# A Trainium2 kernel for one hybrid decoder layer: the heads' stage of the in-projection written out in source order on every engine

## The chip, the cores and the metric

The kernel runs on one core of a Trainium2 chip, as one program. The metric is the device time of one execution in microseconds (us). Before the change three runs took 2206.68 to 2209.07 us, median 2207.49.

The engines are TensorE (PE, matmuls, with PEld for loading its weights), VectorE (DVE), ScalarE (ACT), GpSimd (POOL) and SyncE (SP, which here only issues transfers). Each engine works through its own instructions in their order and waits where an operand isn't there yet.

## What is computed

One layer of a decoder in float32, for a prompt of 512 new tokens and 8 sample tokens that continue older sequences (520 columns in all). D_MODEL is 2048; there are 8 delta heads of dimension 128, and a pooling group 1024 wide. The reference, cut:

```python
proj = rmsnorm(h, norm_mix) @ w_in                 # [q | k | v | z | beta, decay | pool]
qkv_c, new_conv = short_conv(conv_buf, qkv, conv_w)    # 4 taps, then silu
q = l2norm(q) * 128 ** -0.5;  k = l2norm(k)
beta = sigmoid(b_raw);  g = -exp(a_log) * softplus(a_raw + dt_bias)
...
# prompt, in chunks of tokens, per head:
decay = exp(gc_i - gc_j), lower triangle
a_mat = strict_lower((k * beta) @ k.T * decay) + I
u = solve(a_mat, v * beta);  w = solve(a_mat, k * beta * exp(gc))
for each chunk:
    v_new = u - w @ S
    o = (q * exp(g)) @ S + (q @ k.T * decay) @ v_new
    S = S * exp(g_last) + k_dec.T @ v_new
# samples: the same rule token by token, from a given state
dn_out = rmsnorm(o, dn_norm) * silu(z)
pool_out = multiscale_pool(p) @ w_pool * pool_scale
h = h + concat(dn_out, pool_out) @ w_out
h = h + (silu(gate) * up) @ w_down                 # of rmsnorm(h, norm_ffn)
```

## The kernel before

**The products.** A float32 product is taken as three passes over rounded parts (`hi`, and the rest `lo`): hi by hi, hi by lo, lo by hi. The weights come in granules of 128 x 1024 (half of one tile of 128 output columns). `granule` (line 123) loads one by SP into `raw`, ACT rounds it to `hi` (line 135), DVE subtracts to get `lo` (line 137). `product` (line 174) multiplies one tile of weights by all 520 columns in 16 steps of 6 matmuls (lines 170 to 172); the finished sums are taken out of PSUM by DVE in two parts of 264 and 256 columns (`normed_out`, line 261).

**The stages.** First x is loaded, normalized and turned, then come the k tiles 8 to 13 as plain products, the k tiles 14 and 15 and the z tiles 24 to 27 by Strassen's scheme (`strassen`, lines 295 and 301 to 303), then the *heads' stage*: the tiles q h and v 16+h for heads h = 0 to 7, the other z tiles, and eight tiles of the pooling group, one after the other by `product`. In the profile that stage goes from about 172 to 640 us. Behind it follow the out-projection and the feed-forward part.

**What runs beside the products.** After every step of a product `weave.step()` gives a turn to generators in two tracks (class `Weave`, line 43); each yields a number of steps that it wants to wait. The tasks are:

- `states()` (line 1088): rows of the older state, turned by PE and convolved for the samples.
- `keys(h)` (line 1206): of head h the decay `dm` (line 1195, four parts, and Exp), k k^T and the turned k on PE, squares and a power for the norm (line 1203), the matrix `nn` (line 1230; its tile is a row of `mixa` or `mixb`) and `kd` (line 1232).
- `eliminate()` (line 1255): the triangular systems of all heads in one: the diagonal blocks of nn go to DRAM (`nn_d`) and come back as `nb`, one system per partition; 31 pairs of a product and a subtraction on DVE (lines 1269 and 1271), then a turned copy `ut` (line 1274), and both results go to DRAM (`ud_d`, lines 1272 and 1275). `load_u(h)` (line 1187) fetches those of one head as `utf`.
- `delta(h)` (line 1284): from nn and utf to the chain over the chunks: `xp` (line 1304), copy `xt_`, three iterations for `uu` (lines 1323 and 1325), then per chunk `W` (a copy on ACT, line 1365), the products with the state `S` (lines 1354, 1369, 1373) and the output. The q and v of the next head are loaded from DRAM (`c_d`) and convolved while it runs (`take_qv`).
- `gate` (line 1404), and for the samples `sample_norms`, `sample_product(h)` (line 1449; its matmuls, line 1457, read the older state `s`), `sample_out`.

A *convolution* (line 481) is a load, a first product on ACT (line 491), three taps on DVE (line 494) and a silu on ACT (line 496).

**What sets the order.** In the heads' stage PE alone has the order of the source (`manual_schedule(engines={PE})`, line 1028). The other engines' instructions are placed by a scheduler, by priorities; the weights' loads and cuts have a raised one (line 140). The convolutions of heads 2 to 5's keys are placed by hand in the Strassen stage (`early`, `slots`, `after`, line 987), those of 0, 1, 6 and 7 in the heads' stage. `delta(0)` is added to the weave 58 steps behind the start of the elimination (line 1281), each later delta one step behind the one before. The gates of all tokens are worked out in ten pieces in the plain stage (`gates(step)`, line 862); piece 8 is a matmul (line 929) on what DVE writes in piece 7 (`ds_`, line 925, in `mixa`'s room).

## Time and profile before

| | |
|---|---|
| median of three runs | 2207.49 us (2206.68 to 2209.07) |
| the profiled execution | 2204.74 us, its span 2203.0 us, mean granted clock 0.995 |
| PE | 2138.5 us busy, 97% of the span |
| DVE | 1773.2 us, 80% |
| ACT | 960.2 us, 44% |
| POOL | 479.6 us, 22% |

The span goes from the first to the last recorded instruction. The profile gives, for any stretch of it, the busy time of each engine and the granted TensorE clock (1.00 is full speed), and for every instruction what released it: a wait is written as the engine that waits, its operation and line, an arrow, and the engine, tile and line that ended the wait. Line numbers are those of the kernel before.

### The profile page before, as it was taken

To read this page: it belongs to the slowest core of one execution; us is meant where nothing else is said; L and a number is where in the kernel's file an instruction comes from. 1 tells how busy PE (TensorE), PEld (TensorE's weight loads), DVE (VectorE), ACT (ScalarE), POOL (GpSimd) and SP (SyncE) were. 2 spreads that over 40 slices of the span, in tenths; PEclk is the share of its full clock that TensorE was granted. 3 is DMA by queue.
4 is the path that set the end of the run, shared out by engine and by line. 5 is a ranking of instruction groups with operands and counts; after the bars stand their busy time and mean duration, and the time that the engine had idled before them with its cause. 6 is when DMAs were issued, how large, how long until landed. Compare 5 with 4: busy or idle time off the path is not lost.

```text
span 2203.0 us, 43043 instructions
## 1 busy us (share of the span) xinstructions
PE 2138.5 (97%) x17737; PEld 2124.9 (96%) x17737; DVE 1773.2 (80%) x2612; ACT 960.2 (44%) x1470; POOL 479.6 (22%) x600
## 2 busy tenths in 40 slices
PE   7998979999999999999999999999999999999998
PEld 7998979999999999999999999999999999999998
DVE  7788665665569989988888888888887788887997
ACT  6346514443235545443343343443433444435544
POOL 2014312121002210333323323323012402103100
PEclk9999989999999999999999999999999999999999
DMA  8246634432434552554554555555445846447333
GB/s 278 81 139 182 184 112 133 116 107 68 122 107 144 160 159 73 161 152 138 160 154 130 160 153 155 148 149 158 126 119 172 276 107 180 138 109 237 94 109 116
DMA packets 445601, 317.51 MB, mean 144 GB/s; under 512 B 23260, under 2 KB 419957, under 8 KB 442061
## 3 DMA queue, kind: packets, MB, share of 16 engines
q1 hardware_dynamic: 420941, 224.18, 36.3%
q0 software_dynamic: 23296, 89.84, 12.6%
q8 instruction: 139, 2.28, 0.4%
q10 hardware_dynamic: 1168, 0.74, 0.1%
q14 instruction: 57, 0.47, 0.1%
HBM read 261.97 MB, written 53.40 MB: 143 GB/s over the span
## 4 chain that ended last, share of the span: by engine, by line
PE 78%; DVE 10%; DMA 4%; ACT 3%; issue 2%; POOL 1%; ACTq 0%; SPq 0%; DVEq 0%; POOLq 0%
PE dn L301 21%; PE dn L302 21%; PE dn L303 21%; PE mm L170 3%; PE mm L172 3%; PE mm L171 3%; DVE lo L295 2%; DMA vT<-c_d 1%; DVE y L494 1%; ACT hi L294 1%; DVE lo L137 1%; DMA st<-a_d 1%; DVE raw L323 1%; PE dn L1323 0%; DMA mixa<-c_d 0%
## 5 line engine op out<-in xcount | busy, mean ns | idle before, releaser
L294 ACT CAST hi<-raw 128x1024 fp32r<-128x1024 f32 (+1 forms) x447 | 453.2, 1028 | 441.0 <-DVE raw L323 211.1
L295 DVE TENSOR_TENSOR lo<-raw,hi 128x1024 fp32r<-128x1024 f32 (+1 forms) x447 | 558.4, 1268 | 103.1 <-ACT hi L294 101.4
L170 PE MATMUL mm<-xh,hi 128*128 128x264 f32 (+1 forms) x960 | 290.2, 302 | 5.5 <-DVE ext L261 3.4
L172 PE MATMUL mm<-xh,lo 128*128 128x264 f32 (+1 forms) x960 | 272.2, 284 | 1.1 <-DVE lo L137 1.1
L171 PE MATMUL mm<-xl,hi 128*128 128x264 f32 (+1 forms) x960 | 272.0, 283 | 1.3 <-DVE xl L611 1.1
L170 PEld LDWEIGHTS mm<-xh,hi 128*128 128x128 f32 x960 | 182.1, 190 | 6.2 <-DVE ext L261 3.6
L171 PEld LDWEIGHTS mm<-xl,hi 128*128 128x128 f32 x960 | 182.3, 190 | 1.9 <-DVE xl L611 1.9
L323 DVE TENSOR_TENSOR raw<-raw 128x1024 f32<-128x1024 f32 (+1 forms) x136 | 182.2, 1340 | 2.3
L172 PEld LDWEIGHTS mm<-xh,lo 128*128 128x128 f32 x960 | 181.3, 189 | 1.6 <-DVE lo L137 1.6
L302 PE MATMUL dn<-b21l,hi 128*128 128x260 f32 x620 | 175.9, 284 | 0.4 <-DVE b21l L2063 0.4
L303 PE MATMUL dn<-b21h,lo 128*128 128x260 f32 x620 | 175.6, 283 | 0.0
L303 PE MATMUL dn<-b11h,lo 128*128 128x260 f32 x612 | 173.3, 283 | 2.2 <-DVE lo L295 2.2
L301 PE MATMUL dn<-b21h,hi 128*128 128x260 f32 x620 | 175.2, 283 | 0.0
L302 PE MATMUL dn<-b11l,hi 128*128 128x260 f32 x612 | 173.5, 284 | 0.0
L301 PE MATMUL dn<-b11h,hi 128*128 128x260 f32 x612 | 172.9, 283 | 0.0
L301 PE MATMUL dn<-T1h,hi 128*128 128x260 f32 x556 | 158.3, 285 | 0.0
L1685 POOL TENSOR_TENSOR mixa<-mixa 128x520 f32<-128x520 f32 x22 | 51.3, 2332 | 490.7 <-DVE mixa L1679 490.7
L302 PE MATMUL dn<-T1l,hi 128*128 128x260 f32 x556 | 158.0, 284 | 0.0
L303 PE MATMUL dn<-T1h,lo 128*128 128x260 f32 x556 | 156.9, 282 | 0.0
L301 PE MATMUL dn<-B22h,hi 128*128 128x260 f32 x548 | 156.1, 285 | 0.0
L302 PE MATMUL dn<-B22l,hi 128*128 128x260 f32 x548 | 155.9, 284 | 0.0
L303 PE MATMUL dn<-B22h,lo 128*128 128x260 f32 x548 | 154.7, 282 | 0.4 <-DVE lo L295 0.4
(737 smaller groups left out, 6942.0 us busy)
## 6 DMA issues: line engine op xcount, KB each, us to landing
raw<-in_w_gate_up_dram SPq DMA_DIRECT2D x134, 512.0 KB
raw<-in_w_in_dram SPq DMA_DIRECT2D x75, 512.0 KB
a_d<-mixa POOLq DMA_DIRECT2D x22, 1040.0 KB, 5.5
raw<-in_w_down_dram SPq DMA_DIRECT2D x48, 448.0 KB
mixb<-in_w_gate_up_dram SPq DMA_DIRECT2D x41, 512.0 KB
raw<-in_w_out_dram SPq DMA_DIRECT2D x25, 512.0 KB
st<-a_d POOLq DMA_DIRECT2D x49, 260.0 KB, 6.5
raw<-in_w_down_dram SPq DMA_DIRECT2D x24, 512.0 KB
```

Source lines behind the costliest of these rows:

```text
L137: dve.tensor_tensor(lo[:, r], raw[:, r], hi[:, r].bitcast(F32), op=ALU.subtract)
L170: te.matmul(acc[ci], wh, hi[k][:, c0:c1], start=(i == 0), stop=False)
L171: te.matmul(acc[ci], wh, lo[k][:, c0:c1], start=False, stop=False)
L172: te.matmul(acc[ci], wl, hi[k][:, c0:c1], start=False, stop=(i == len(w) - 1))
L294: act.copy(hi, raw)
L295: dve.tensor_tensor(lo, raw, hi.bitcast(F32), op=ALU.subtract)
L301: te.matmul(acc, wh[:, k, :], xf[:, k, :], start=start and k == 0, stop=False)
L302: te.matmul(acc, wh[:, k, :], xg[:, k, :], start=False, stop=False)
L303: te.matmul(acc, wl[:, k, :], xf[:, k, :], start=False, stop=stop and k == wh.shape[1] - 1)
L323: dve.tensor_tensor(r[name], r[a], r[b], op=op)
L494: return lambda: dve.scalar_tensor_tensor(ys[0], x[:, i:i + SEQ], cw(i, t), ys[0], op0=ALU.mult, op1=ALU.add)
L1685: pool.tensor_tensor(q[:, 4:8:2, :], q[:, 1:4:2, :], q[:, 0:2, :], op=ALU.subtract)
```

## The change

1. **Source order on every engine** for the heads' stage up to its 23rd tile: `manual_schedule()` without a list of engines. The last five pooling tiles stay as they were.
2. **A clock for tasks.** `Weave` gets `at(step, task)`, a task that starts at a given step (a step is six matmuls of a product), and `feed`, called at every step.
3. **Weights by step.** Granule n is used from step 8n on; its load is issued at step 8(n−3), its cut (hi on ACT, lo on DVE) at step 8n−10.
4. **Keys as staged tasks**, from the steps in `KS`, about 11 apart: each with its own convolution, then decay, silu and Exp, matmuls, squares, power, nn, with yields between. The early convolutions in the Strassen stage go. The blocks are stored by SP and fetched into `nb` head by head (`nd_d`), not by POOL in two halves.
5. **The elimination** starts at step 104 and is spread with yields over about 40 steps; the results of head 0 are stored first, `load_u(0)` comes four steps behind.
6. **Deltas** from step 154 (`D0`), 26 steps each, one behind the other. The load of the next head's q is issued at the start of a delta, that of v two steps later; Exp of dm comes behind the copy xt_. The gate is a task of its own.
7. **Samples:** `sample_product` takes 6 steps per head in place of 8. **Gates:** pieces 8 and 9 come one step later.
8. `kept_d` holds nn of heads 4 to 7 too, the decay rows are loaded ahead (`load_decay`), and some buffers are shared differently (pooling's `pw` and splits).

The diff, cut to its core:

```diff
+KS, ELIM, D0 = (-5, 8, 21, 33, 44, 55, 66, 77), 104, 154
...
     def step(self):
         self.now += 1
+        if self.feed:
+            self.feed(self.now)
+        for x in list(self.single):
+            if self.now >= x[0]:
+                n = next(x[1], None)
...
             elif step == 8:
+                pass
+            elif step == 9:
                 te.matmul(bank("e")[:, 0:128], ones[:NB, :], ds_.rearrange("p a b -> p (a b)"), start=True, stop=True)
...
+        def feed(now):
+            if (now + 10) % 8 == 0 and (now + 10) // 8 >= 2:
+                feed_cut((now + 10) // 8)
+            if now % 8 == 0:
+                feed_load(now // 8 + 3)
...
-        early = [convolution(places(h)[0], 8 + h, lambda k=k: mixa[:, 6 + k % 2, 0:SEQ]) for k, h in enumerate((2, 3, 4, 5))]
...
         def keys(h):
             x, nn = places(h)
             kT = x[:, 3:3 + SEQ]
+            conv = convolution(x, 8 + h, y_tile)
+            conv[0]()
+            load_decay(h)
+            yield 5
+            for f in conv[1:4]:
+                f()
+                yield 1
+            conv[4]()
+            yield 1
             _, dm = decay(h)
+            yield 1
+            conv[5]()
+            act.activation(dm, dm, AF.Exp)
+            yield 3
             gp_ = pst()
...
+            yield 2
             ss = d1tile("ss", [P, NCH], "ss")
             squares(ktp, ss)
+            yield 2
...
-            pool.dma_start(nn_d[:, NCH * h:NCH * h + NCH], nn.rearrange("p (n r j) -> p n r j", n=NCH, r=4))
+            for q in range(4):
+                r = slice(32 * q, 32 * q + 32)
+                sp.dma_start(nd_d[h, q].rearrange("c s j -> s c j"), nn3[r, :, r])
...
+            yield 4
+            if not nbs:
+                nbs.append(d1tile("nb", [P, 32, 32], "nb"))
+            sp.dma_start(nbs[0][16 * h:16 * h + 16].rearrange("p s j -> p (s j)"),
+                         nd_d[h].rearrange("q c s j -> (q c) (s j)"))
...
+                work += 0.34 + t * w / 480
+                if work > 0.55:
+                    yield int(work / 0.55)
+                    work %= 0.55
...
+            yield 4
+            load_u(0)
+            yield 4
+            load_u(1)
...
         def delta(h):
...
+                to_come = take_qv(h + 1)
+                to_come.pop(0)()
...
             act.copy(xt_, v3(xp)[:, :, 0:96])
+            act.activation(dm, dm, AF.Exp)
...
+            weave.at(weave.now + 1, gate(h, op_, fq, nn))
...
+                    if j != 1:
+                        yield 1
...
+        with tc.high_priority(offset=8 * AHEAD), tc.manual_schedule():
+            weave.feed = feed
+            weave.add(states())
+            for h in range(H):
+                task = keys(h)
+                if KS[h] < 0:
+                    weave.at(KS[h] + next(task), task)
+                else:
+                    weave.at(KS[h], task)
+            weave.at(ELIM - 12, first_qv())
+            weave.at(ELIM - 6, eliminate())
...
+            weave.at(D0 - 8, deltas())
```

How this stands on the engines, at three places. Line numbers in the rows after are those of the changed kernel: line 275 is `normed_out`, 308 and 309 the cuts hi and lo, 505, 508 and 510 a convolution's first product, taps and silu.

DVE from nn of head 7 (L1230) to the elimination's first pair (L1269, L1271) before:

```order
L1230 SCALAR_TENSOR_TENSOR mixa<-dn,sck,dm 128x128 x4
L1232 TENSOR_TENSOR kd<-dn,sck 128x512
L137 TENSOR_TENSOR lo<-raw,hi 128x1024
L1298 TENSOR_TENSOR qts<-qT,gcb 128x512
L1195 SCALAR_TENSOR_TENSOR dm<-gcb,gcs,mneg 128x128 x3
L261 TENSOR_TENSOR ext<-mm,rb 128x264
L1195 SCALAR_TENSOR_TENSOR dm<-gcb,gcs,mneg 128x128
L261 TENSOR_TENSOR ext<-mm,rb 128x256
L137 TENSOR_TENSOR lo<-raw,hi 128x1024 x2
L261 TENSOR_TENSOR ext<-mm,rb 128x264
L1269 TENSOR_TENSOR tm<-nb,u 128x31
L1271 TENSOR_TENSOR u<-u,tm 128x31
```

And after (nn is L1255, the first pair L1291 and L1293; L1248 to L1251 are the norm's small operations):

```order
L1248 TENSOR_TENSOR sck<-rr 128x4
L1249 TENSOR_TENSOR sck<-ss,rr 128x4
L1250 TENSOR_TENSOR sck<-sck,btok 128x4
L1251 TENSOR_TENSOR sck<-sck,edec 128x4
L1255 SCALAR_TENSOR_TENSOR nn<-dn,sck,dm 128x128 x4
L1257 TENSOR_TENSOR kd<-dn,sck 128x512
L508 SCALAR_TENSOR_TENSOR y<-qT,prm,y 128x512 x3
L508 SCALAR_TENSOR_TENSOR y<-vT,prm,y 128x512
L309 TENSOR_TENSOR lo<-raw,hi 128x1024
L508 SCALAR_TENSOR_TENSOR y<-vT,prm,y 128x512 x2
L1291 TENSOR_TENSOR tm<-nb,u 128x31
L1293 TENSOR_TENSOR u<-u,tm 128x31
```

The first operations of head 0's delta (qts and dm) are no longer ahead of the elimination; the six taps for head 0's q and v now stand there.

DVE at the start of head 1's delta before (L1389 to L1394 are the end of head 0's, L1325 is uu of the first iteration):

```order
L1298 TENSOR_TENSOR qts<-qT,gcb 128x512
L1195 SCALAR_TENSOR_TENSOR dm<-gcb,gcs,mneg 128x128 x4
L1389 TENSOR_TENSOR so<-so,ro 128x4
L1390 TENSOR_SCALAR so<-so 128x4
L1392 TENSOR_TENSOR ro<-ro,fq 128x4
L1394 TENSOR_TENSOR mixb<-dn,ro 128x512
L1325 SCALAR_TENSOR_TENSOR uu<-dn,utf_2094 96x4x96
L137 TENSOR_TENSOR lo<-raw,hi 128x1024
```

And after (uu is L1377):

```order
L1203 SCALAR_TENSOR_TENSOR dm<-gcb,gcs,mneg 128x128 x4
L1366 TENSOR_TENSOR qts<-qT,gcb 128x512
L309 TENSOR_TENSOR lo<-raw,hi 128x1024
L1377 SCALAR_TENSOR_TENSOR uu<-dn,utf_2068 96x4x96
L1383 TENSOR_SCALAR ss<-ss 128x4
L1387 SCALAR_TENSOR_TENSOR aq<-dn,sck,dm 128x128 x4
```

The cut lo, which stood behind the first uu, now stands ahead of it, and the end of head 0's delta has left this place.

ACT at the same place after (Exp of gcb, the copy xt_, Exp of dm, the squares of q and of head 0's output, and the cut hi, which the lo above reads):

```order
L1350 ACT_TABLE_LOAD
L1350 ACTIVATE gcb<-gcb 128x512
L1358 COPY xt__4182<-dn 128x384
L1359 ACTIVATE dm<-dm 128x512
L1210 ACTIVATE junk,ss<-dn 128x128 x4
L1210 ACTIVATE junk,so<-dn 128x128 x4
L308 CAST hi<-raw 128x1024
```

The hi stands behind eight squares there.

More of the change, by code (lines that the diff above doesn't have):

```diff
@@ L1022, in decoder_kernel @@
         nparts[0][1](dve)
+        for n in range(2, 4):
+            feed_load(n)
         xas.close()
@@ L1196, in decay @@
                                          op0=ALU.subtract, op1=ALU.min)
-            act.activation(dm, dm, AF.Exp)
             return gcb, dm
@@ L1379, in delta @@
                 S = S2
+                if c == 2 and h + 1 < H:
+                    load_decay(h + 1)
                 more()
@@ L1391, in delta @@
             pow_mhalf(ro, so)
+            yield 3
             dve.tensor_tensor(ro, ro, fq, op=ALU.mult)
-            on = nn
             dve.tensor_tensor(v3(on), v3(op_), bc3(ro), op=ALU.mult)
-            if h + 2 < H:
-                load_u(h + 2)
-            if h + 1 < H:
-                weave.add(delta(h + 1), 0, 1)
-            else:
-                for task in (conv_out(), sample_norms(), *map(sample_product, range(H)), sample_out()):
-                    weave.add(task)
-            weave.add(gate(h, on), 1, 8)
-        def gate(h, on):
+            yield 2
+            while h >= 4 and 24 + h not in traced:
+                yield 1
             otp = pst()
@@ L1421, in sample_norms @@
         def sample_norms():
-            take = scratch("nb", "u")
+            take = scratch("aq", "vs", "qts")
             smp["take"] = take
@@ L1539, in pool_tile, with pooled @@
             product(w, xhk, xlk, evict)
+            for _ in pooled(t, pe0, operands):
+                if weave.now <= SPLIT:
+                    pass
+        def pooled(t, pe0, operands):
+            gi = t // 2
+            win = 2 << gi
             pool.tensor_copy(pcp[:, :, t], pe0[:, 512:527])
@@ L1585, in pool_out @@
             sp.dma_start(np_prompt[0, 0].rearrange("j (t p) -> (j t) p", p=P), st[:120, :])
-        kds = {}
-        for h in range(2):
-            take_k(h)
-        weave.add(states())
-        for h in (2, 3, 0, 1, 4, 5, 6, 7):
-            weave.add(keys(h), 1)
-        for h in range(H):
-            qkv_tile(h, None if h else w_next)
-            qkv_tile(16 + h)
-            for z in {6: (4, 5), 7: (6, 7)}.get(h, ()):
-                z_tile(z)
+        SPLIT = 16 * 23
         splits = {}
```

237 lines of the change are left out of this document (132 added, 105 removed).

## Prediction

> **What bounds the kernel now.** I read the stretches of the span first (columns: length, busy time of PE, PE's weight load, DVE, ACT and POOL in us with their instructions, granted TensorE clock, DMA share, GB/s):
>
> ```profile
> 100.00:140.00 40.00, 38.91 (x325) 38.61 (x324) 35.82 (x50) 17.69 (x20) 9.65 (x21) 1.00 0.47 144
> 140.00:180.00 40.00, 33.53 (x250) 31.76 (x249) 32.91 (x53) 18.80 (x32) 3.68 (x9) 0.96 0.41 119
> 180.00:250.00 70.00, 64.00 (x534) 63.06 (x533) 55.59 (x160) 45.53 (x103) 33.13 (x67) 1.00 0.70 198
> 250.00:296.00 46.00, 46.00 (x384) 45.87 (x383) 32.74 (x76) 15.59 (x19) 8.59 (x18) 1.00 0.49 138
> 296.00:320.00 24.00, 9.37 (x69) 9.19 (x68) 11.19 (x34) 1.95 (x9) 3.15 (x7) 0.72 0.31 85
> 320.00:560.00 240.00, 230.11 (x1967) 226.31 (x1966) 143.29 (x320) 101.70 (x250) 41.63 (x93) 1.00 0.40 109
> 560.00:640.00 80.00, 77.77 (x655) 77.34 (x654) 40.60 (x94) 21.82 (x32) 2.58 (x9) 1.00 0.42 114
> 640.00:700.00 60.00, 56.80 (x465) 55.78 (x464) 59.20 (x96) 32.24 (x51) 7.11 (x10) 1.00 0.45 133
> 700.00:2203.00 1503.00, 1493.22 (x12402) 1491.75 (x12400) 1288.46 (x1564) 654.03 (x853) 353.73 (x332) 1.00 0.50 148
> ```
>
> TensorE bounds the whole program: after 700 us it idles 1503.00 − 1493.22 = 9.8 us, and the change leaves that part alone. Its matmuls stay the same in number and size, so the change can only win idle PE time. From 100 to 700 us that is 1.1, 6.5, 6.0, 0, 14.6, 9.9, 2.2 and 3.2 = 43.5 us. A clock below 1.00 adds to it: 0.04 × 40 = 1.6 us of lost work in 140–180, and behind the big gap this stretch:
>
> ```profile
> 311.00:317.00 6.00, 5.48 (x33) 5.51 (x34) 0.56 (x2) 1.95 (x9) 1.90 (x3) 0.61 0.20 32
> ```
>
> 0.39 × 5.48 = 2.1 us. So about 47 us stand in the stages that the change rewrites. The full row 250–296 also gives a unit: 46.00 us for 384 matmuls, so one step of the weave (6 matmuls) is 0.72 us.
>
> Next, the waits of PE, each stretch by itself (who waits, for whom: total us, times, longest):
>
> ```profile
> PE mm L929 <- DVE mixa L925: 1.1, 1, 1.1
> ...
> PE dn L303 <- DVE lo L295: 2.8, 5, 0.7
> PE mm L170 <- ACT hi L135: 2.2, 1, 2.2
> ...
> PE mm L170 <- DVE ext L261: 3.4, 1, 3.4
> ...
> PE dn L1304 <- DMA utf<-ud_d: 14.6, 1, 14.6
> PE dn L1369 <- ACT W L1365: 5.2, 6, 1.5
> PE dn L1354 <- DVE S L1373: 3.3, 5, 1.0
> ...
> PE dn L1457 <- DMA s<-in_state_delta_dram: 2.2, 2, 1.7
> ```
>
> The largest is one wait: the first delta matmul waits for the result of the elimination. Those for W and S come from ACT, which itself stands still in the delta stage for a late load:
>
> ```profile
> ACT y L491 <- DMA vT<-c_d: 26.0, 6, 6.9
> ```
>
> **The change, term by term.** *Gates.* Their matmul moves one step back, behind the DVE work that it waits for: the 1.1 us goes, **−1.1**.
>
> *End of the Strassen pairs (140–180 us; 6.5 idle, 1.6 clock).* The four early convolutions leave. Their prices (start, duration, engine, line, operation):
>
> ```profile
> 324.55 0.73 ACT L491 ACTIVATE y<-vT,prm 128x512 f32<-128x512 f32 x1 [3.38 <-DMA vT<-c_d]
> 325.18 0.25 ACT L1365 COPY W<-dn 128x128 f32<-128x128 f32 x1
> 327.72 1.28 ACT L496 ACT_TABLE_LOAD   x1 [2.29 <-DVE y L494]
> 329.01 0.63 ACT L496 ACTIVATE vT<-y 128x512 f32<-128x512 f32 x1
> 330.43 1.54 DVE L494 SCALAR_TENSOR_TENSOR y<-qT,prm,y 128x512 f32<-128x512 f32 x2 [1.66 <-ACT y L491]
> ```
>
> Twelve taps of 1.54/2 = 0.77 us are 9.2 us off a DVE that is busy 32.91 of 40, and ACT loses four first products and silus that stand between cuts; the waits for lo and hi there (2.8 + 2.2) lose their cause in part. But the first granules of the heads' stage must be cut there too. I take **−3**; bounds 0 and −8.
>
> *Keys (180–250 us; 6.0 idle, 3.4 of it PE waiting for an eviction).* The convolutions that left come here, so every head of about 11 steps has its own. Rows for the sum, the cut and eviction by groups (busy, mean ns of one | idle before):
>
> ```profile
> 342.94 1.14 DVE L1195 SCALAR_TENSOR_TENSOR dm<-gcb,gcs,mneg 128x128 f32<-128x128 f32 x4
> ...
> 257.74 1.12 DVE L1230 SCALAR_TENSOR_TENSOR mixa<-dn,sck,dm 128x128 f32<-128x128 f32 x4
> 258.77 0.68 DVE L1232 TENSOR_TENSOR kd<-dn,sck 128x512 f32<-128x512 f32 x1
> ...
> 315.26 0.28 ACT L1203 ACTIVATE junk<-dn 128x128 f32<-128x128 f32 x1
> 315.66 0.28 ACT L1203 ACTIVATE junk<-dn 128x128 f32<-128x128 f32 x1
> 320.13 1.05 ACT L135 CAST hi<-raw 128x1024 fp32r<-128x1024 f32 x1 [4.10 <-PE mm L171]
> ```
>
> ```profile
> L137 DVE TENSOR_TENSOR lo<-raw,hi 128x1024 fp32r<-128x1024 f32 x4 | 4.9, 1220 | 0.0
> L261 DVE TENSOR_TENSOR ext<-mm,rb 128x264 f32<-128x264 f32 x2 | 0.9, 430 | 1.1 <-PE mm L172 1.1
> ```
>
> Of the chain of waits, the keys' own product on PE:
>
> ```profile
> 233.63 0.89 PE dn L1215 x8
> ```
>
> DVE per head: three taps 2.3, decay 1.14, nn 1.12, kd 0.68, small operations 0.5 (my guess), and 11/8 of a cut (1.22) and of an eviction (0.43) 2.3: 8.0 us. PE per head: 11 × 0.72, the product 0.89 and four transposes, about 0.5 by half of that product's eight: 9.3 us. ACT: two table loads 2.6, silu and Exp 1.3, first product 0.73, four squares at a pitch of 315.66 − 315.26 = 0.40, 1.6, and 11/8 of a hi cut 1.4: 7.6 us. Both fit under PE, without much slack, and in source order a late square now holds the next hi, and that holds lo. On SP the first load of blocks waits until the states' scratch in the same buffer is free, with weight loads queued behind it; those run 24 steps (17 us) ahead of use, which covers a wait of some us. I take **−2**; bounds −6 (all idle time goes) and +8 (1 us per head: an eviction wait like the 3.4 in every third).
>
> *Elimination gap (14.6 idle + 2.1 clock).* Before:
>
> ```profile
> 275.41 0.20 DVE L1269 TENSOR_TENSOR tm<-nb,u 128x31 f32<-128x31 f32 x1
> ...
> 303.88 1.03 DVE L1274 COPY ut<-u 128x1024 f32<-128x1024 f32 x1
> ...
> 311.52 1.99 PE L1304 MATMUL dn<-utf,mixb 128*128 128x96 f32 x8 [14.63 <-DMA utf<-ud_d]
> ```
>
> The elimination takes 303.88 − 275.41 = 28.5 us; four lo cuts (4.9) and three evictions (1.3) lie in it, so its own 62 instructions take 22.3. The copy ut is 1.03; store and load up to the first matmul 311.52 − 304.91 = 6.6. After: keys of head 7 start at step 77 and their matmuls come at step 90, delta(0) at 154, so PE has 64 × 0.72 = 46.0 us of other work plus the keys' matmuls 1.4: 47.4 us. The chain in that time: matmuls 1.4, squares 1.6, one hi 1.05 and one lo 1.22 ahead in order, power 1.05 (as hi), small operations 0.5, nn 1.12, and the DRAM round trip of the blocks 6.6 (as that of u): 14.5. Then elimination 22.3 with five cuts (6.1) and five evictions (2.1) among it, 30.5; ut 1.0; round trip 6.6. (The six taps for head 0, 4.6 us, that now stand ahead of the elimination in DVE's order, fit into the blocks' round trip.) Together 52.6, so a gap of 52.6 − 47.4 = 5.2, with perhaps 1.5 of clock. 16.7 − 6.7 = **−10**; bounds −6 (four stores and a load of blocks per head leave POOL's queue for SP's and stand there between weight loads) and −16.7.
>
> *Delta stage (320–560; 9.9 idle).* q's load is issued at the delta's start and v's two steps later, so ACT no longer stands 26.0 us for them, and most of 5.2 + 3.3 goes: −8. What comes: in heads 1 and 5 a cut is due at the delta's start, so lo waits for hi, which stands in ACT's order behind eight squares, and DVE's uu of the first iteration stands behind lo. On ACT eight squares at 0.40 and hi 1.05 are 4.3; with Exp, the xt_ copy, the table load and lo 1.22 lo ends some 7.8 us after the start and uu at 8.2. PE wants uu here:
>
> ```profile
> 343.65 1.03 PE L1304 MATMUL dn<-utf,mixb 128*128 128x96 f32 x8
> ...
> 349.45 0.81 PE L1323 MATMUL dn<-uu,xt__4035 128*96 128x64 f32 x8
> ```
>
> 349.45 − 343.65 = 5.8 us, so about 2.4 us twice; some 0.8 in head 3, and 0.5 for pooled rows in head 7: +6. Net **−2**; bounds −8 and +6.
>
> *Sample heads (560–640; 2.2 idle).* Each takes 6 steps in place of 8, so the state loads have 1.4 us less per head. At one of the two waits the transfer was this long (chain of waits):
>
> ```profile
> 581.30 5.09 DMA s<-in_state_delta_dram
> ```
>
> They were just late twice; two steps less make a few of the eight late: **+1.5**; bounds 0 and +6 (0.7 each).
>
> Sum: −1.1 − 3 − 2 − 10 − 2 + 1.5 = −16.6. The profiled execution took 2204.74 us, so 2188.1; the median of the runs shown, 2207.49, lies 2.75 above it, so **2191**.
>
> A rule that could speak against the change concerns table loads: keys now alternate silu, Exp and power. In the rows above a load takes 1.28 us, and the ACTIVATE at 329.01 begins as it ends (327.72 + 1.28), with no time between. The Trainium skill ("ScalarE: Activation LUTs", section "What ACT_TABLE_LOAD costs") gives about 1.28 us for the load and a further 1.38 us for a drain at every switch; the first agrees with the row, the second doesn't show behind it, and by it the sum would be rival D's.
>
> **The rivals.** *A, nearly all waits go* (0.15). The blocks' round trip is short, the cuts come in time: −1.1 − 5 − 5 − 14 − 7 + 0 = −32, so 2175; with every idle us to 640 and the clock 2163. For it: the step numbers leave 50 steps from elimination to delta. Against: the chain above is longer than its cover by my rows.
> *B, the gain is given back* (0.10). The elimination ends as late as before relative to PE (−2 in place of −10), keys cost 4, samples 3, Strassen's end −2, delta −2: about 0, so 2207–2208. For it: DVE and ACT keep their total work.
> *C, slower: cuts in strict order starve PE* (0.06). Each of the 46 granules from the feed can come late when its hi stands behind an ACT instruction that waits for PE. From (16.6 + 4.4)/46 = 0.46 us each it decides for slower; 0.8 us each gives +37 − 16.6 = +20, 2228. Against: a cut runs ten steps (7.2 us) ahead of use.
> *D, table switches drain* (0.03). If each of two switches per key head cost ACT another 1.28, its 7.6 become 10.2 against PE's 9.3: 0.9 × 8 = +7, so 2198. For it, only the rule; the row at 329.01 speaks against.
> The forecast has 0.66.
>
> **Numbers.** A measurement of this kernel can tell about 0.2%, 4.4 us. Faster (under 2203.1): forecast 0.64, A and D 0.18, so 0.82. Same: B's most and the forecast's upper end, 0.10. Slower: C and B's rest, 0.08. The forecast's own range, from the terms with two or three of them at an end, is 2178–2203; to hold 8 in 10 it reaches half way into A, to 2172, and to B's lower part, 2206.
>
> **What would show it.** In the profile after: the wait of delta's first matmul for utf at about 5 us, not 14.6 (A: under 1; B: over 12); no ACT wait for vT over 1 us; PE waiting for uu in heads 1 and 5 at about 2.4 us; no PE wait of over 1 us for lo or hi in the keys. Wrong would be: matmul waits for lo or hi in tens (C), or ACT idle over 1 us behind each table load (D).

## The result, and the profile after

The changed kernel takes 2236.23 us (median of 4 runs, 2234.43 to 2238.40) against 2208.28 for the kernel before, run beside it: ratio 1.0126, 95% interval 1.0108 to 1.0144. It is slower by 28 us, where 2191 was forecast. Its profiled execution took 2237.41 us, span 2235.7, mean granted clock 0.987 (before 0.995). The two profiled executions lie 32.7 us apart, 4.7 more than the medians, since that of the kernel before is faster than its median and this one slower; what follows explains the 32.7.

Engines' busy time on the page of the changed kernel:

```profile
PE 2153.5 (96%) x17737; PEld 2139.6 (96%) x17737; DVE 1771.9 (79%) x2612; ACT 970.4 (43%) x1476; POOL 480.2 (21%) x596
```

The span grew by 32.7 us. PE's idle time grew from 2203.0 − 2138.5 = 64.5 to 2235.7 − 2153.5 = 82.2, by 17.7 us. The other 15.0 us are *busy* time: the same 17737 matmuls took longer. The stretches tell why (columns as in the prediction; the clock is the third number from the end):

```profile
140.00:180.00 40.00, 36.82 (x302) 35.99 (x301) 30.57 (x48) 20.22 (x38) 6.50 (x11) 1.00 0.41 114
180.00:250.00 70.00, 53.20 (x399) 52.20 (x399) 41.84 (x113) 31.43 (x61) 19.90 (x45) 0.88 0.43 119
250.00:296.00 46.00, 39.11 (x307) 38.02 (x305) 28.69 (x73) 26.35 (x50) 19.45 (x49) 0.96 0.67 200
296.00:320.00 24.00, 21.80 (x166) 21.80 (x167) 22.66 (x55) 4.13 (x5) 2.94 (x6) 0.87 0.30 90
320.00:560.00 240.00, 214.40 (x1754) 211.14 (x1753) 128.18 (x290) 97.00 (x225) 37.38 (x74) 0.94 0.40 112
```

Before, the clock stood below 1.00 only behind the elimination gap, once in 140–180 and at the very end. Now it is at 0.88 among the keys and 0.94 over the whole delta stage, where it was 1.00. Times shift between the kernels, so the stages are better compared by a place in the work, the start of the same tile's first matmul. For the first tile of the heads' stage, before and after:

```profile
173.48 0.39 PE L170 MATMUL mm<-xh,hi 128*128 128x264 f32 x1 [2.18 <-ACT hi L135]
```

```profile
165.58 0.39 PE L184 MATMUL mm<-xh,hi 128*128 128x264 f32 x1 [0.52 <-ACT hi L149]
```

The table gives this for more tiles (from the traces, us; the elimination's gap lies between v 3 and q 5 in both). The last three columns split the stage's difference: PE's idle time, the work lost at half clock (half of PE's busy time in the records at 0.50), and the rest.

| first matmul of | before | after | difference | this stage | forecast | idle | half clock | rest |
|---|---|---|---|---|---|---|---|---|
| q 0 (end of Strassen's pairs) | 173.5 | 165.6 | −7.9 | −7.9 | −4.1 | −5.9 | 0.0 | −2.0 |
| v 3 (keys) | 276.2 | 291.7 | +15.5 | **+23.4** | −2 | +17.3 | +5.2 | +0.9 |
| q 5 (elimination) | 337.3 | 351.9 | +14.6 | −0.9 | −10 | −0.3 | +2.8 | −3.3 |
| end of the span (deltas, samples, rest) | 2203.0 | 2235.7 | +32.7 | **+18.1** | −0.5 | +6.6 | +8.2 | +3.3 |

The rest in the last two rows is work that changed its place: between v 3 and q 5 PE has 338 matmuls after and 366 before, since more of head 0's delta now comes behind q 5. So the elimination's −0.9 hides a loss: by idle time and clock the stage is 2.5 us worse. The −2.0 in the first row stays open.

**Among the keys** PE's waits after (180 to 320 us: total, times, longest):

```profile
PE dn L1234 <- ACT mixb L510: 16.8, 3, 9.3
PE dn L1234 <- ACT mixa L510: 4.6, 3, 3.0
PE mm L184 <- DVE ext L275: 3.8, 1, 3.8
```

L1234 is the keys' product, L510 the silu of the key's convolution. The convolution is late from its first step. For head 1 the timeline of the changed kernel shows (POOL, ACT, DVE; in brackets the idle time ahead and what ended it):

```profile
174.02 0.76 POOL L1088 DMA_DIRECT2D nt<-in_state_conv_dram  x1 [20.81 <-DVE lo L151]
...
177.42 0.59 POOL L501 DMA_DIRECT2D mixb<-c_d  x1
...
184.87 0.72 ACT L505 ACTIVATE y<-mixb,prm 128x512 f32<-128x512 f32 x1 [5.05 <-DMA mixb<-c_d]
...
186.57 1.23 DVE L309 TENSOR_TENSOR lo<-raw,hi 128x1024 fp32r<-128x1024 f32 x1 [4.57 <-ACT hi L308]
187.71 0.75 DVE L508 SCALAR_TENSOR_TENSOR y<-mixb,prm,y 128x512 f32<-128x512 f32 x1
...
192.64 1.28 ACT L510 ACT_TABLE_LOAD   x1 [6.10 <-DVE y L508]
```

Read it downwards: POOL stood 20.8 us ahead of a load for `states`, until the last Strassen cut (L151) was done; the key's load (L501) is behind it in POOL's order and goes out at 177.42. ACT starts on it at 184.87; ACT, waiting for it, does the next hi cut late; DVE waits for that hi with lo, and the taps stand behind lo. The silu starts at 193.9 and PE waits 6.5 us. For head 3 it is POOL again, waiting for an eviction:

```profile
213.50 0.19 POOL L492 COPY ccp<-ext 128x3 f32<-128x3 f32 x1 [4.67 <-DVE ext L275]
...
215.64 0.54 POOL L501 DMA_DIRECT2D mixb<-c_d  x1
...
221.88 0.72 ACT L505 ACTIVATE y<-mixb,prm 128x512 f32<-128x512 f32 x1 [6.52 <-DMA mixb<-c_d]
```

Two things add up here. The source has head 3's load at step 33, which PE ended at 208.0: it went out 7.6 us late. Head 1's load (step 8, ended at 176.2) went out only 1.2 us late, but ACT had the data 7.4 us after the issue, and its use, five steps on, was due at 181.5. The lead of five steps is itself short: by the profile's list of transfers the keys' loads from 166 to 292 us take 6.2 us into `mixb` and 5.0 into `mixa` from issue to landing (medians), and five steps of PE without a gap are 3.6 us.

**At the elimination** the wait for utf is 10.8 us, not 14.6 and not 5.2. DVE's copy ut, and SP behind it:

```profile
323.88 1.11 DVE L1299 COPY ut<-u 128x1024 f32<-128x1024 f32 x1
```

```profile
323.92 0.68 SPq L1303 DMA_DIRECT2D ud_d<-u  x1
325.02 0.63 SPq L1303 DMA_DIRECT2D ud_d<-ut  x1
325.70 0.85 SPq L1303 DMA_DIRECT2D ud_d<-u  x1
326.59 0.80 SPq L1303 DMA_DIRECT2D ud_d<-ut  x1
327.49 2.57 SPq L300 DMA_DIRECT2D raw<-in_w_in_dram  x1
330.12 2.56 SPq L1196 DMA_DIRECT2D gcb<-gcr_d  x1
332.79 7.66 SPq L1192 DMA_DIRECT2D utf<-ud_d  x8
```

The loads of head 0's results stand behind the stores of the other heads, a weight load and a decay load. They begin 7.8 us after ut is done (324.99); the first delta matmul comes at 340.9, 15.9 us after it, where before it was 6.6.

**In the deltas** the forecast cut shows. Head 1 (the first two rows are the first and the last of the eight squares):

```profile
374.42 0.27 ACT L1210 ACTIVATE junk<-dn 128x128 f32<-128x128 f32 x1
...
377.21 0.28 ACT L1210 ACTIVATE junk<-dn 128x128 f32<-128x128 f32 x1
...
377.48 1.04 ACT L308 CAST hi<-raw 128x1024 fp32r<-128x1024 f32 x1
...
378.55 1.22 DVE L309 TENSOR_TENSOR lo<-raw,hi 128x1024 fp32r<-128x1024 f32 x1 [4.29 <-ACT hi L308]
379.69 0.55 DVE L1377 SCALAR_TENSOR_TENSOR uu<-dn,utf 96x384 f32<-96x384 f32 x1
```

PE's waits there (340 to 560 us; the row for utf, the gap above, and the smallest are left out; all but utf come to 14.8 us):

```profile
PE dn L1375 <- DVE uu L1377: 5.1, 3, 3.0
PE dn L1416 <- DVE R L1411: 2.6, 2, 2.2
PE dn L1408 <- DVE S L1429: 2.1, 2, 1.3
```

### The profile page after: what moved, and what is told of

It is laid out like the page before. It is cut to its first block, busy times and chain, and to the rows that moved or that the text cites. A ratio compares the mean times of both kernels' runs of the same rounds, so it can differ in the third digit from the quotient of the medians.

```text
span 2235.7 us, 43054 instructions
## 1 busy us (share of the span) xinstructions
PE 2153.5 (96%) x17737; PEld 2139.6 (96%) x17737; DVE 1771.9 (79%) x2612; ACT 970.4 (43%) x1476; POOL 480.2 (21%) x596
## 4 chain that ended last, share of the span: by engine, by line
PE 67%; DVE 5%; ACT 2%; issue 1%; DMA 1%; POOL 0%; ACTq 0%; DVEq 0%; POOLq 0%
PE dn L316 20%; PE dn L315 20%; PE dn L317 20%; PE mm L184 1%; DVE lo L309 1%; PE mm L186 1%; PE mm L185 1%; DMA s<-in_state_delta_dram 1%; ACT hi L308 1%; DMA st<-a_d 1%; PE dn L1511 0%; DVE raw L337 0%; PE mm L315 0%; PE mm L316 0%; PE mm L317 0%
## 5 line engine op out<-in xcount | busy, mean ns | idle before, releaser
L309 DVE TENSOR_TENSOR lo<-raw,hi 128x1024 fp32r<-128x1024 f32 (+1 forms) x493 | 613.1, 1261 | 140.4 <-ACT hi L308 138.7
L308 ACT CAST hi<-raw 128x1024 fp32r<-128x1024 f32 (+1 forms) x493 | 501.2, 1029 | 464.0 <-DVE raw L337 218.1
L184 PEld LDWEIGHTS mm<-xh,hi 128*128 128x128 f32 x960 | 187.0, 195 | 6.0 <-DVE ext L275 4.0
L186 PEld LDWEIGHTS mm<-xh,lo 128*128 128x128 f32 x960 | 185.9, 194 | 3.7 <-DVE lo L151 2.7
L185 PEld LDWEIGHTS mm<-xl,hi 128*128 128x128 f32 x960 | 187.0, 195 | 1.9 <-DVE xl L620 1.9
```

The lines of the kernel that those rows point to most:

```text
L184: te.matmul(acc[ci], wh, hi[k][:, c0:c1], start=(i == 0), stop=False)
L185: te.matmul(acc[ci], wh, lo[k][:, c0:c1], start=False, stop=False)
L186: te.matmul(acc[ci], wl, hi[k][:, c0:c1], start=False, stop=(i == len(w) - 1))
L308: act.copy(hi, raw)
L309: dve.tensor_tensor(lo, raw, hi.bitcast(F32), op=ALU.subtract)
```

## The experiments

All times are medians, but for three single runs (head 0's q and v later, the gates alone, the stalls); the kernel before, run beside each, took 2206.6 to 2208.4. Differences of one or two us between medians are within the spread of the runs (the changed kernel's four span 4 us). Edits are to the changed kernel unless said. A "half-clock piece" is 3.41 us of the granted clock at 0.50; a record of it lasts one such piece or several. Waits are the profile's idle times; the recorded expectations take some of them from start to start of the matmuls around, which gives 0.1 to 0.2 us more.

### Loads of the keys earlier

```diff
             conv[0]()
+            yield 8
             load_decay(h)
...
-                if KS[h] < 0:
-                    weave.at(KS[h] + next(task), task)
+                if h < 2:
+                    weave.at(KS[h] - 8 + next(task), task)
                 else:
-                    weave.at(KS[h], task)
+                    weave.at(KS[h] - 8, task)
```

> Edit to the changed kernel: the load of each key's convolution is issued 8 steps earlier (13 steps ahead of its first product in place of 5), so that the first two stand on POOL's queue ahead of the states' loads. Theory (late loads): in the changed kernel PE waits 22.4 us for keys' silus, and loses 10.2 us of clock behind three of these waits, because each convolution's load stands in POOL's order behind instructions that wait (20.8 us once, then copies and clears of 4 to 9 us). Then these waits fall under 6 us and the time falls by 20 to 28 us, to about 2208 to 2216. Rival (order on DVE: taps of the next head stand behind nn of the head before, which waits for the power on POOL): at least 14 us of the waits stay, time above 2225.

2216.73 us, 19.5 less than the changed kernel, at the edge of what the theory gave (20 to 28). PE's waits for silus, by the waits of this run:

```profile
PE dn L1235 <- ACT mixa L510: 5.4, 4, 3.2
PE dn L1235 <- ACT mixb L510: 4.2, 2, 2.9
```

They fell from 21.4 to 9.6 us, not under 6, and from three half-clocked places among the keys one is left. Late loads are the larger part: no first product waits for a load any more. The 9.6 us that stay are the rival's: in the four longest the third tap stands on DVE behind operations for nn of the head before, which in the two longest of all (2.9 and 3.2 us) had waited for the power on POOL, and in some a tap also stands behind a lo. (The 10.2 us of clock in the expectation count six whole pieces; in the changed kernel PE was busy in part of them only and lost 6.9 among the keys.)

### The other heads' results stored by POOL

```diff
-                    sp.dma_start(ud_d[hs, :, a]...
+                    (pool if hs.start else sp).dma_start(ud_d[hs, :, a]...
```

> Edit to the changed kernel: the elimination's results of heads 1 to 7 are stored by POOL's queue; SP keeps those of head 0 and then the loads. Theory (the loads of head 0's results stand behind the other heads' stores, a weight load and a decay load in SP's queue, which issued in 0.85, 0.80, 2.57 and 2.56 us): from the end of ut to the first delta matmul it takes 8 to 10 us in place of 15.8, the gap of 10.8 falls to 3 to 5 and the time by 6 to 10 us, to 2226 to 2230. Rival (the DRAM round trip itself became slower by its smaller pieces): the gap stays at 10 to 11, no change in time (within 3 us).

2231.85 us, 4.4 less; the gap fell from 10.8 to 7.5. A weight load and the decay load (1.47 and 1.21 us of issue here) still stand ahead of utf, whose loads begin 4.9 us after ut in place of 7.8. The direction was right; the size was about half, and the gap stayed above the 3 to 5 us expected.

### Squares behind the cut

```diff
-            squares(qtp, ss)
             fq = d1tile("fq", [P, NCH], "fq")
             yield 2
+            squares(qtp, ss)
...
-            weave.at(weave.now + 1, gate(h, op_, fq, nn))
+            weave.at(weave.now + 4, gate(h, op_, fq, nn))
```

> Edit to the changed kernel: in each delta the four squares of q come two steps later, behind the first iteration's matmuls, and the gate's four squares three steps later, so that no squares stand on ACT between the copy xt_ and the next hi cut. Theory (lo waits for hi behind eight squares, and uu waits behind lo): PE's waits for uu fall from 8.9 us in all to about 3, two or three of the half-clock periods (1.7 us each) go, and the time falls by 6 to 12 us, to 2224 to 2230. Rival (the in-order cut only moves on: the same lo then holds R, W or S): time within 3 us of 2236.

2228.52 us, 7.7 less. From this run's waits (340 to 560 us):

```profile
PE dn L1408 <- DVE S L1427: 2.4, 3, 1.1
...
PE dn L1375 <- DVE uu L1377: 0.2, 1, 0.2
```

In this stretch the wait for uu in its first iterations is gone (5.1 to 0.2); 2.0 us of it moved to the first S (0.4 to 2.4). Head 7's, behind 560 us, stays at 2.1. Of four half-clocked places in the deltas two are left, and a new one stands behind head 7's wait, each with a single piece. So lo behind squares was a cause, at about the size expected.

### The deltas by the scheduler

```diff
+            tiles_(0, 9)
+        with tc.high_priority(offset=8 * AHEAD), tc.manual_schedule(engines={mybir.EngineType.PE}):
+            tiles_(9, 20)
             pool_tiles((4, 5, 6), 20)
```

`tiles_(a, b)` is the loop over the stage's tiles a to b − 1.

> Edit to the changed kernel: source order on all engines only up to the ninth tile (keys and most of the elimination); from the tenth on, with all deltas, PE alone is in source order, as in the kernel before, and the others go by the scheduler. Theory (strict order of cuts, taps and chain on ACT and DVE makes PE wait in the deltas): from the first delta to the end of the samples 12 to 20 us go, time 2216 to 2224. Rival (the waits come from the deltas' pace, 26 steps back to back, and from later loads, not from the order): at least three quarters of the waits stay, time above 2230.

2214.75 us, 21.5 less. Gap and deltas (325 to 560 us):

```profile
PE dn L1356 <- DMA utf<-ud_d: 3.5, 1, 3.5
PE dn L1416 <- DVE uu L1377: 3.0, 4, 1.7
PE dn L1375 <- DVE uu L1377: 0.9, 1, 0.9
```

With the same tasks at the same steps PE's waits in the deltas fall from 14.8 to 5.4 us in all. The gap falls by 7 us: on SP the loads of utf now follow the four stores at once, 2.5 us after ut, and the weight loads come behind them.

### Head 0's q and v later

```diff
-            weave.at(ELIM - 12, first_qv())
+            weave.at(ELIM + 8, first_qv())
```

> Edit to the changed kernel: the convolutions of head 0's q and v come at step 112, among the elimination's pairs, in place of step 92 ahead of its first pair. Theory (their taps, which wait for late loads and for ACT, hold DVE's order ahead of the elimination and of two evictions): the elimination starts 3 us earlier with respect to the keys of head 7, and PE's waits of 0.9 and 3.9 us just ahead of it, for a lo and an eviction, go: 6 to 9 us in all, with half-clock periods. Rival (the blocks' round trip ends there anyway): the elimination starts at most 1 us earlier, and only the eviction waits move.

2240.86 us, 4.6 more: a miss. An eviction wait of 8.5 us stands there now (295 to 340 us):

```profile
PE mm L184 <- DVE ext L275: 8.5, 1, 8.5
```

ACT waited 13.0 us for the load of q in this run; the taps on DVE waited for ACT, and the eviction stood behind the taps. The load of q still came four steps ahead of use. The elimination's first pair did come 4.4 us earlier (14.3 us behind the start of head 7's product, 18.7 in the changed kernel), as the theory had it, but with the taps among its pairs its copy ut came 4.7 us later (53.0 and 48.3 us behind that product). Moving the consumers moved the stall.

### Loads of q and v earlier, elimination and deltas later

```diff
-KS, ELIM, D0 = (...), 104, 154
+KS, ELIM, D0 = (...), 110, 160
...
-                yield 1
+                yield 11 if i == 3 else 1
...
-            weave.at(ELIM - 12, first_qv())
+            weave.at(82, first_qv())
```

> Edit to the changed kernel: the loads of head 0's q and v are issued 10 steps earlier (their first products stay where they were), and the elimination and the deltas start 6 steps later (110 and 160). The run with these taps at step 112 showed the eviction waits only moved, so the theory is now: in source order DVE's evictions stand behind operations that wait for a load (taps for q and v, the elimination's first pair for its blocks). With both loads in time, PE's waits of 0.9 and 3.9 us ahead of the elimination and 3.4 us of clock go, and the gap ahead of the first delta falls from 10.8 us to 5 to 8, since PE has 4.3 us more of other work: 8 to 14 us in all, 2222 to 2228. Rival (the elimination is bound by its own order among cuts and evictions): the eviction wait goes but the gap stays, time above 2230.

2238.38 us, no gain. The eviction wait fell (from 3.8 us), the gap hardly did (from 10.8 us; 280 to 345 us):

```profile
PE dn L1356 <- DMA utf<-ud_d: 9.8, 1, 9.8
PE mm L184 <- DVE ext L275: 2.0, 2, 1.6
```

The rival holds for the gap: the load of the last blocks was issued at 285.4 us and the first pair ran at 294.1, with DVE busy, or waiting for ACT with a tap of v and a lo, in between; the elimination is bound by its own order. The deltas, now at another phase against the cuts (every 8 steps), had longer waits, the longest 4.6 us for uu and 3.8 for S. That a shift of six steps does this looks like the same cause; it wasn't tried alone.

### Edits together

> All the edits that helped together, on the changed kernel: loads of the keys' convolutions 8 steps earlier, the elimination's results of heads 1 to 7 stored by POOL, head 0's q and v at step 112, the deltas' stage by the scheduler on all engines but PE. If the losses are separate, the gains add: 2236.2 less 19.5, 4.4, 21.5 and some 3 to 6 is 2185 to 2188, below the kernel before by 0.9 to 1.0%. If they share a cause (a wait that only moves), it stays above 2200.

2215.50 us. The gains did not add: the later q and v, a loss by itself, brought two eviction waits of 13.5 us together, as it had brought one of 8.5 by itself. Without it and without the store by POOL:

> The two edits that gained most, together on the changed kernel and without the others: key loads 8 steps earlier, and the deltas' stage by the scheduler on all engines but PE. If the two losses are separate the gains add, 2236.2 less 19.5 and 21.5, to 2193 to 2199, faster than the kernel before; if the eviction waits that the run of all edits showed belong to one of these two, it stays above 2205.

2199.25 us, ratio to the kernel before 0.9960 (0.9948 to 0.9972). Added, the two edits would give 2195.2, so they are separate up to 4 us; the time lies at the upper edge of what was expected. With the later elimination on top:

> The two edits of the run before this one and the two of the run with the later elimination (q's and v's loads 10 steps earlier, elimination and deltas 6 steps later). By the same theories the eviction waits ahead of the elimination go too: 3 to 8 us less than the two edits alone, 2187 to 2195. Rival (the scheduler had already filled these waits): within 2 us of the two edits alone.

2205.42 us, 6.2 worse: neither theory had that sign. Its trace has a wait of 5.8 us in the deltas, for the output of a gate, that the run without it lacks; why the scheduler made it wasn't tried.

### Source order undone on all engines but PE

```diff
-        with tc.high_priority(offset=8 * AHEAD), tc.manual_schedule():
+        with tc.high_priority(offset=8 * AHEAD), tc.manual_schedule(engines={mybir.EngineType.PE}):
             weave.feed = feed
```

> The changed kernel with one thing undone: source order on all engines. PE alone is in source order, the others go by the scheduler, as in the kernel before; tasks, steps, queues, loads and buffers stay those of the change. Theory (the loss is the strict order of ACT, DVE, POOL and SP, in which one late load holds everything behind it): the 28 us by which the change is slower go, and some of the forecast gain shows: 2190 to 2206. Rival (the loss is in the new steps and places, such as a key's load 5 steps ahead of use and 26 steps for each delta): time above 2220.

2191.97 us, 44.3 less than the changed kernel, ratio to the kernel before 0.9927 (0.9915 to 0.9939). It is the fastest version of this study. Its waits from 180 to 320 us, all of them:

```profile
PE dn L1356 <- DMA utf<-ud_d: 6.2, 1, 6.2
PE mm L184 <- DVE ext L275: 5.0, 4, 3.3
PE dn L1100 <- DVE mixb L1255: 3.4, 1, 3.4
```

No key waits for a silu, and in SP's order the same four stores are followed by utf at once:

```profile
307.08 0.80 SPq L1303 DMA_DIRECT2D ud_d<-ut  x1
307.98 5.58 SPq L1192 DMA_DIRECT2D utf<-ud_d  x8
```

By tiles it stands at −8.0 at q 0, −3.6 at v 3, −14.7 at q 5 and −13.8 at the end of the span: stages of −8.0, +4.4, −11.1 and +0.9. Here too 3.1 us of the −11.1 are work that moved behind q 5, so that waits and clock account for −8.0 there.

Which engines' order? One run kept it on DVE and ACT, the other on POOL and SP (and both on PE):

```diff
-        with tc.high_priority(offset=8 * AHEAD), tc.manual_schedule():
+        with tc.high_priority(offset=8 * AHEAD), tc.manual_schedule(engines={mybir.EngineType.PE, mybir.EngineType.DVE, mybir.EngineType.Activation}):
             weave.feed = feed
```

> The changed kernel with source order kept on PE, DVE and ACT, and the queues' engines POOL and SP given to the scheduler. The run with all four given to it took 2192.0 us, that with all four in source order 2236.2. Theory A (the loss sits mostly in the transfers' order on POOL and SP: late loads, stores ahead of loads): most of the 44 us go, below 2210. Theory B (it sits mostly in the order of cuts, taps, evictions and chain on ACT and DVE): less than half go, above 2214.

2213.73 us, 22.5 less: half of the 44.3. PE's waits among the keys (175 to 270 us) fell by half, from 21.4 to 10.9 us, while those of the deltas stayed (7.3 us at the matmuls that read uu, 2.6 for R, 2.1 for S):

```profile
PE dn L1234 <- ACT mixb L510: 7.4, 3, 3.4
PE dn L1234 <- ACT mixa L510: 3.5, 3, 1.7
```

> The converse: source order kept on PE, POOL and SP, the scheduler orders DVE and ACT. Theory A: less than half of the 44 us go, above 2214. Theory B: most go, below 2210. If both this and the run before stay above 2214, the two orders hold each other's work up and only both together free it.

2223.38 us, 12.9 less. Late loads remain (175 to 340 us), with the queues in source order:

```profile
PE dn L1356 <- DMA utf<-ud_d: 14.1, 1, 14.1
PE dn L1234 <- ACT mixb L510: 10.1, 2, 8.5
```

Neither theory alone: the queues' order costs more, the compute engines' less, and some 9 us go only when both are free (44.3 − 22.5 − 12.9; with four medians in it, this last figure is good to a few us).

> The key loads 8 steps earlier, with all engines but PE given to the scheduler. In source order this edit gained 19.5 us. If the scheduler already issues the loads in time, it gains nothing here (2188 to 2195); if a key's load 5 steps ahead of use is too late by itself, it gains 3 us or more, below 2189.

2193.08 us, no gain over 2191.97. So with the scheduler the lead of five steps costs nothing. That does not clear the lead in source order: there the step fixes the place in POOL's list, and the edit that gained 19.5 us changed both, the lead and the place ahead of the loads for `states`. How the 19.5 us divide between the two wasn't tried.

### The gates alone, on the kernel before

```diff
             elif step == 8:
+                pass
+            elif step == 9:
                 te.matmul(bank("e")[:, 0:128], ones[:NB, :], ...
...
         def after(q, j):
 
+            if (q, j) == (0, 1):
+                gates(10)
```

> One part of the change alone, on the kernel before: the gates' matmul and the copy behind it one step later. Theory: PE's wait of 1.1 us for them goes and nothing else moves, so the first tile of the heads' stage starts 1 to 1.5 us earlier, and the remaining 6.5 us of the 7.9 us by which it starts earlier in the changed kernel belong to the early convolutions that left. Rival: the gates hold more than their wait (the work behind them on DVE), and 3 us or more go.

2206.46 us, a difference too small to tell in the time; the place in the work shows it. No wait of PE is left from 100 to 140 us, and q 0 starts 1.0 us earlier. About as expected; the other 6.9 of the 7.9 us come with the rest of the change up to that place, of which the early convolutions are the part that ran there (by difference, not tried alone).

### What a stall costs, on the kernel before

```diff
+    def stall(n):
+        t = pst()
+        te.transpose(t[:, 0:P], ident, ident)
+        act.copy(ident, t[:, 0:P])
+        for i in range(n):
+            act.copy(ident, ident)
+        te.transpose(t[:, P:2 * P], ident, ident)
+
     def hidden(q, j):
+        if j == 4 and 4 <= q < 28:
+            stall((1, 3, 5, 7, 10, 14)[q % 6])
```

> Added to the kernel before, in the feed-forward part, where PE has no gap: 24 small chains of a transpose on PE, 2, 4, 6, 8, 11 or 15 copies on ACT and a transpose that waits for them (four of each length), so that PE stands for about 0.8 to 5 us at known places. The computed values stay the same. Theory (a stall costs its own time and one or more half-clock periods of 3.41 us, 1.7 us of work each, once it is over about 2 us): no period behind the stalls under 1.5 us, one behind most of those of 2 to 4 us, two or more behind longer ones, and the time is the sum of the gaps and about 25 to 35 us more. Rival (only stalls over 3.4 us lose clock): periods behind the longest four or eight alone, 7 to 20 us more than the sum of the gaps.

2349.06 us, 142.5 more, from gaps that add up to 91.5 us: 51 us more than the gaps. Of these, 43.6 are the work lost in the half-clock pieces; the 48 transposes themselves are in the rest. The granted clock around a gap of 1.34 us at 1054, and around one of 2.67 us at 1103:

```profile
1054.00:1056.00 2.00, 0.66 (x7) 0.43 (x5) 1.45 (x4) 1.37 (x5) 0.00 (x0) 1.00 0.69 206
1056.00:1058.00 2.00, 2.00 (x18) 2.00 (x18) 2.00 (x2) 0.74 (x1) 0.00 (x0) 1.00 0.00 0
...
1104.00:1106.00 2.00, 0.19 (x2) 0.19 (x2) 1.56 (x2) 1.84 (x7) 0.00 (x0) 0.82 0.03 8
1106.00:1108.00 2.00, 2.00 (x10) 2.00 (x10) 1.23 (x1) 0.70 (x1) 0.00 (x0) 0.50 0.52 153
```

Behind the second, PE does 10 matmuls in 2 us where it does 18 behind the first. All 24, from the clock's records:

| gap, us | half-clock pieces of 3.41 us, four gaps each |
|---|---|
| 1.34 | 0, 0, 0, 0 |
| 2.67 | 1, 1, 1, 1 |
| 3.21 | 2, 2, 1, 1 |
| 4.53 | 1, 1, 2, 2 |
| 4.97 | 1, 2, 2, 2 |
| 6.17 | 2, 2, 2, 3 |

The theory holds in the main: 32 pieces and more time than it expected, though three of the eight gaps of 4.5 to 5.0 us drew one piece and not two. The rival, that only gaps over 3.4 us lose clock, falls.

## Why the prediction was wrong, point by point

- **The step that failed** is in the keys: "Both fit under PE, without much slack." The terms compared busy times per head (8.0 and 7.6 us under 9.3), and of what can be late in order they asked for the *cuts* and, on SP, the first load of blocks. POOL's list isn't in them. In source order a load's issue is also an instruction with a place: the loads of heads 1 to 3 went out 1.2, 8.1 and 7.6 us behind their steps, with a lead of five steps that was short besides; ACT and DVE waited for them, and whatever stood behind waited too. Forecast −2, bounds to +8; measured +23.4. With order free the same stage is +4.4, inside the bounds.
- **The clock's price of short stalls** was left out. The forecast charged it for the big gap alone. Of the 32.7 us, about half are matmuls at half clock (15.0 by busy time, 16.2 by the clock's records); the table of stalls gives one piece for 2.67 us, and delta waits of 1.6 to 3.0 us drew one or two in four places.
- *Elimination:* forecast −10, measured −0.9, and +2.5 by idle time and clock alone. From the start of head 7's product it took 18.7 us to the first pair (forecast 14.5), 29.6 to ut (30.5), 1.1 for ut (1.0) and 15.9 for the round trip (6.6); PE's cover was 54.6 us (47.4): 65.3 − 54.6 = 10.7. So the mis-sized term is "round trip 6.6": the two loads that stand between in SP's order, and the stores of the other heads, made it 15.9. The taps that "fit into the blocks' round trip" did not: they wait for ACT and for late loads, and with them moved away the first pair came at 14.3. The cover is longer because PE itself stood in it, 0.8 us for a lo and 3.8 for an eviction, which stood behind these taps on DVE, and ran two pieces at half clock. With order free the gap is 6.2, where 5.2 was forecast.
- *Deltas:* the late vT went, as forecast. The uu waits of heads 1 and 5 were put at 2.4 each and measured 1.9 and 3.0, by the cause given. But heads 3 and 7 took 1.6 and 2.1 where 0.8 and 0.5 were forecast, the waits for W and S fell only from 8.5 to 5.7 us (all heads) where 8 were to go, R cost 2.6, and 8.2 us of clock came on top.
- *Samples:* +1.5 was forecast; PE's waits for s are 1.3 us after, 2.2 before. No loss.
- *End of Strassen's pairs and gates:* −4.1 forecast, −7.9 measured, inside the bounds (−9.1 to −1.1 for both together).
- *Rivals:* C had the sign and nearly the time (2228), for another reason, so this is luck: PE waits for few cuts (0.8 us for a lo, ahead of the elimination). D, the drain at table switches, doesn't show: the silu of head 1 starts at 193.93 behind a load from 192.64 of 1.28. B had the elimination nearly right (−2 against −0.9), and not the keys.

The sum as forecast, −16.6, comes close to the change *without* its first sentence: with only PE in source order the profiled span is 13.8 us shorter than before, and the median is 2191.97 where 2191 was forecast. That it comes so close is in part luck, since the first two stages miss in opposite directions (−8.0 for −4.1, +4.4 for −2). Source order itself costs 44.3 us, and the prediction priced it at some 6, in the deltas.

## What to carry to other kernels

Before all engines are put in source order, walk each queue's list and ask of every instruction that can wait, a transfer's issue above all, what stands behind it: averages of busy time say nothing on that. Issue loads ahead of anything that waits on the same engine, and keep small urgent stores and loads free of bulk loads between them. Count a stall of PE with its clock: in the run with stalls those of 2.67 us cost 1.4 to 1.7 us more each; a gap that falls across two of the clock's windows (see below) can cost nothing more.

## What the runs showed of the hardware

- The granted clock falls to 0.50 in pieces of 3.41 us. No piece came behind isolated gaps of 1.34 us, one behind each of 2.67 us. In between it varied: gaps of 1.90, 2.18 and 1.58 us in the deltas drew one piece each in the changed kernel, and the same three waits (1.90, 2.17, 1.56) none in the run with earlier key loads. The Trainium skill ("TensorE: Matmul & The Clock Gate", section "HAM oscillation — how this bites in real kernels") sets the rule at idle gaps over about 3.4 us; here shorter ones cost clock too, and the measurement decides. Its section "What's actually happening" says that the window of 3.413 us runs freely; that would explain why equal gaps differ, and the length agrees, but no run here sets the phase.
- The traces bear this out. In each of the 17, all half-clock pieces lie a whole number of 3.413 us apart, on one grid. PE's idle time counted by the windows of that grid (from 100 us to 30 us before the end): of the windows at full clock, all 101 with 1.9 us or more were followed by a half-clock piece, 17 of 71 with 1.4 to 1.9 us, and 2 of the other 10028. Behind a half-clock piece another one followed in 82 of 82 cases with 0.7 us of idle time or more in it, and in 5 of 125 with less. So it matters how a gap falls: the three delta waits lay in one window each, almost wholly, in the changed kernel and across two in the run with earlier key loads, and the kernel before has a gap of 3.36 us (to 228.70) that is split 1.58 and 1.78 and drew no piece.
- In SP's list a weight load and a decay load took 2.57 and 2.56 us to issue right behind four stores (1.47 and 1.21 behind two, with the other stores on POOL), where such issues mostly take 0.3 to 0.6 us elsewhere in the same list. The issue of a transfer is not always short; why it wasn't here is open.
